# State-space output of a hybrid encoder block, computed transposed in column halves of TensorE

## The chip, the cores and the metric

The kernel runs on one core of a Trainium2 chip. The metric is the device time of one execution in microseconds (us). TensorE (PE, with its weight loads PEld), VectorE (DVE), ScalarE (ACT), GpSimd (POOL) and SyncE (SP, which issues most transfers) run side by side and wait for each other through semaphores.

## The reference

One encoder block over 1024 tokens of width 1024: RMS norm, a product with `w_in`, two groups of heads side by side (a Mamba-2 state-space group, "SSD", and a stick-breaking attention group), a product with `w_out`, norm and residual, then a SwiGLU mixer (`w_gate`, `w_up`, `w_down`). What the change touches is the SSD's output:

```python
y_diag = jnp.einsum("bgcls,bgrcls,bcsgrp->bclgrp", cb, decay_in, x)      # within a block
y_off = jnp.einsum("bclgn,bcgrpn,bgrcl->bclgrp", cc, prev, jnp.exp(a_cs)) # from the state before it
y = y_diag + y_off + d_skip[:, None] * xs
```

There are 8 heads of 64 channels, in two groups of four; a group shares B and C with 128 states. The kernel works in 8 blocks of 128 tokens rather than the reference's 16 of 64, which gives the same sums.

## The kernel before, in words

All arrays are float32. Large products run as three products of split operands (`mm3`, L76 to L78, float32r). The products of the SSD are plain float32, and each appears in the trace as two matmul records and two weight loads.

The program is written as generators. `attention` is one stream of small steps (scores L561 and L562, sigmoids L563 and L564, a scan L567, transposes L578, splits L582 and L583, products with the values L590). `fill` is the other: it goes through `PLAN`, in which tiles of `w_in`'s product (`proj`) alternate with conv tiles, and from "ssd" on it takes one step of `ssd()` behind each step of `proj`. `merge` interleaves the two streams by the costs that each step yields (TensorE us, VectorE us). Program order is only a priority: the framework that builds the kernel orders the instructions of each engine ahead of time by its own model of when each would be ready, and each engine, SP's queue of transfers among them, then runs its list strictly in order. Tiles come from pools with a fixed number of places per tag: `t2` has 8 places of 2 KB for a partition, used by the SSD, by q, k and v on their way to DRAM, by attention's `otmp` and `vld`; the PSUM tag `px` has 3 banks, used by the SSD, attention's transposes and the norms.

`dt_stage` makes, among others, `acs` (running sums of the decay exponents, tokens on partitions), their exponential `E_c`, and a transposed copy `acsT` (rows are block and head, columns are tokens), which goes to DRAM as `acs_d` and comes back broadcast to all partitions as `ab`.

`ssd()` has `front(b)` for a block: it loads `cx` (8 channel tiles of x, B, C by 128 tokens) and the decay matrix `de`, makes C times B in `pcb` (L416), transposes B (L418) and x (L429), multiplies the decay in (`Gm`, L423: per head, source tokens on partitions, target tokens along the free axis) and x by dt (`xdt`, L431: tokens by channels). A block then has three steps. Step A: eight products for `py` (L441, stationary `Gm`, moving 64 columns of `xdt`), `xdc` (L445), two products for `po` (L449, stationary C of a group, moving 256 columns of the state), `y = po * E_c` (L450), `y += py` (L451); the first block has no state and copies `py` with ACT (L453). Step B: `front` of the next block. Step C: the new state (`pst` L460, L463, L467), then `yd = cx * dsk` by four ACT instructions (L473), four transposes of `y` into `pyt` (L476), `yd += pyt` (L477), and the store to `ys_d` (L478). The `z` tiles load `ys_d` later and gate it.

Of the kernel before, what the change touches and what calls it, by code (L numbers as in the profile page):

```python
# [16 lines left out]
P = 128  # L17
S = 1024
# [16 lines left out]
# what in_proj makes, in order; "ssd" from where on SSD's steps run beside the tiles  # L35
PLAN = ('qkv1', 'x0', 'x1', 'x2', 'x3', 'x4', 'x5', 'qkv2', 'x7', 'x6', 'ssd', 'qkv3', 'z0', 'z1', 'r0', 'z2', 'z3', 'wo', 'l1', 'o0')
# how far attention is where the other stream is 0, 1/8, .. 1 done
# [10 lines left out]
def tile_hybrid_block(  # L48
# [15 lines left out]
    """The rows of x and out run backwards in time (row s is token S-1-s), so that every  # L64
    running product over earlier tokens is a forward scan along the free axis."""
# [4 lines left out]
    def split(hi, lo, src):  # L70
        """hi + lo == src, hi and lo each exact in float32r."""
        A.copy(hi, src)  # L72
        V.tensor_tensor(lo, src, f32(hi), ALU.subtract)  # L73
# [6 lines left out]
    # ------------------------------------------------------------------ constants  # L80
# [20 lines left out]
    # TensorE's clock rises with use: products of ones while the first loads run  # L101
# [3 lines left out]
    # tri[s, l] = 1 where s >= l  # L105
    tri = const.tile([P, P], F32, name="tri")
    G.affine_select(tri, ones_f, [[-1, P]], ALU.is_ge, 0.0, base=0, channel_multiplier=1)
    # scan floor: 1 where the key is not strictly before the query, 0 elsewhere
# [3 lines left out]
    # column h is 1 on the 64 partitions of head h of a pair  # L112
# [6 lines left out]
    E_c = const.tile([P, NB, NH], F32, name="E_c")  # L119
# [4 lines left out]
    # DRAM scratch  # L124
    cx_d = dram.tile([8, P, S], F32, name="cx_d")
    dec_d = dram.tile([NB, P, NH * P], F32, name="dec_d")
    acs_d = dram.tile([NB * NH, P], F32, name="acs_d")
    ys_d = dram.tile([4, P, S], F32, name="ys_d")
    y_d = [dram.tile([8, P, 512], F32, name=f"y_d{n}") for n in range(2)]
    # means of squares and what they make 1 / rms: even heads, odd heads, SSD groups  # L130
# [8 lines left out]
    # ------------------------------------------------------------------ right side: x * gain and in_proj weights  # L139
# [4 lines left out]
    # the rows' 1 / rms scales columns here, so it is applied to what comes out of in_proj  # L144
# [13 lines left out]
    # sel16 sums the products of the two halves of w2  # L158
# [11 lines left out]
    # columns of w_in in the order of their use; each tile is loaded and split while the one before it  # L170
    # is multiplied
# [5 lines left out]
    def fetch_w(half=None):  # L177
        """The next column tile, or one half of it."""
# [15 lines left out]
    # ------------------------------------------------------------------ pre-mix norm, first products  # L194
# [40 lines left out]
    # ------------------------------------------------------------------ left side: attention, conv and SSD work  # L235
# [20 lines left out]
    def qkv_tiles(j, st):  # L256
        """What takes q, k (each in its two parts) and v of a pair of heads out of PSUM, to DRAM."""
# [38 lines left out]
    # ------------------------------------------------------------------ dt, decays  # L296
    def dt_stage():
# [18 lines left out]
        # softplus(x) = max(x, 0) + log1p(exp(-|x|)), log1p(e) = 2 atanh(e / (2 + e))  # L316
# [23 lines left out]
        A.activation(E_c, acs, AF.Exp)  # L340
# [6 lines left out]
        nc.sync.dma_start(acs_d, acsT)  # L347
        yield
# [11 lines left out]
        # attention's sigmoids, which need these, wait for the last exponential: ScalarE changes its table once  # L360
# [4 lines left out]
    # ------------------------------------------------------------------ conv tiles  # L365
# [38 lines left out]
    # ------------------------------------------------------------------ SSD  # L404
    def ssd():
# [27 lines left out]

        cur = front(NB - 1)
        yield 1.6, 1.8
        for b in range(NB - 1, -1, -1):
            sl = slice(P * b, P * b + P)
            cx, bs, Gm, xdt = cur
            py = psum("px", "py", [P, 512])
            for h in range(NH):  # L440
                T.matmul(py[:, HD * h : HD * h + HD], lhsT=Gm[:, h, :], rhs=xdt[:, h, :], start=True, stop=True)  # L441
# [4 lines left out]
            if state is not None:  # L446
                po = psum("px", "po", [P, 512])
                for g in range(2):
                    T.matmul(po[:, 256 * g : 256 * g + 256], lhsT=cx[:, 6 + g, :], rhs=state[:, 256 * g : 256 * g + 256], start=True, stop=True)  # L449
# [922 lines left out]
```

## Time and profile before

| | us |
|---|---|
| median of 3 runs | 1248.95 |
| lowest, highest run | 1248.57, 1249.61 |
| span of the profiled execution | 1249.6 |
| TensorE busy in it | 1204.2 (96%) |
| VectorE busy in it | 932.1 (75%) |
| ScalarE busy in it | 587.7 (47%) |

The span is from the first to the last instruction of the profiled execution; it lies at the upper end of the three runs and 0.65 us over their median, so nothing has to be added around it. Busy TensorE time counts pipelined matmuls from start to modelled end, and a busy engine is not one at its peak. The chain of work followed back from the last instruction is 69% TensorE, 14% VectorE and 8% transfers.

### The profile page before, as it was taken

To read this page: it belongs to the slowest core of one execution; us is meant where nothing else is said; L and a number is where in the kernel's file an instruction comes from. 1 tells how busy PE (TensorE), PEld (TensorE's weight loads), DVE (VectorE), ACT (ScalarE), POOL (GpSimd) and SP (SyncE) were. 2 spreads that over 40 slices of the span, in tenths; PEclk is the share of its full clock that TensorE was granted. 3 is DMA by queue.
4 is the path that set the end of the run, shared out by engine and by line. 5 is a ranking of instruction groups with operands and counts; after the bars stand their busy time and mean duration, and the time that the engine had idled before them with its cause. 6 is when DMAs were issued, how large, how long until landed. Compare 5 with 4: busy or idle time off the path is not lost.

```text
span 1249.6 us, 16320 instructions
## 1 busy us (share of the span) xinstructions
PE 1204.2 (96%) x5641; PEld 972.0 (78%) x5641; DVE 932.1 (75%) x1461; ACT 587.7 (47%) x1115; POOL 92.1 (7%) x232
## 2 busy tenths in 40 slices
PE   8998999999999998998799999999999999999997
PEld 7776778787887776787678888888888888888885
DVE  7478988778997887676897565566555558998777
ACT  7347655556655666444653332333233325444543
POOL 0041110010110100011200000000000000000000
PEclk9998999999999999999899999999999999999999
DMA  5693252445466326754872212312132198133336
GB/s 188 194 358 107 67 152 82 142 117 178 142 181 190 118 93 212 228 173 159 271 207 93 93 60 93 101 59 93 52 100 98 58 327 318 62 124 101 102 135 235
DMA packets 139882, 183.23 MB, mean 147 GB/s; under 512 B 10660, under 2 KB 94852, under 8 KB 139800
## 3 DMA queue, kind: packets, MB, share of 16 engines
q1 hardware_dynamic: 128544, 151.18, 38.3%
q0 software_dynamic: 7424, 25.17, 5.5%
q10 hardware_dynamic: 3832, 5.84, 1.3%
q8 instruction: 44, 0.72, 0.2%
q14 instruction: 38, 0.31, 0.1%
HBM read 132.23 MB, written 49.92 MB: 146 GB/s over the span
## 4 chain that ended last, share of the span: by engine, by line
PE 69%; DVE 14%; DMA 8%; issue 4%; ACT 4%; SPq 2%; DVEq 0%; ACTq 0%
PE pd L77 5%; PE pd L76 5%; PE pd L78 5%; DVE sn L567 3%; DMA Rb<-r_d 3%; PE o L590 2%; PE tp L578 2%; PE pj_x L76 2%; PE pj_x L78 2%; PE pcg L76 2%; PE pj_x L77 2%; PE pcu L76 2%; PE peg L76 2%; PE peu L76 2%; PE peu L77 2%
## 5 line engine op out<-in xcount | busy, mean ns | idle before, releaser
L72 ACT CAST flhi<-fraw 128x512 fp32r<-128x512 f32 x102 | 62.7, 622 | 174.1 <-PE pcg L77 37.0
L77 PE MATMUL pd<-folo,fohi 128*128 128x512 f32 x260 | 101.2, 389 | 0.0
L76 PE MATMUL pd<-fohi 128*128 128x512 f32 x260 | 101.2, 389 | 0.0
L78 PE MATMUL pd<-fohi,folo 128*128 128x512 f32 x260 | 101.1, 389 | 0.0
L567 DVE TENSOR_TENSOR_SCAN sn<-sn,smask 128x1024 f32<-128x1024 f32 (+3 forms) x64 | 87.4, 1366 | 17.7 <-ACT sn L563 17.7
L73 DVE TENSOR_TENSOR fllo<-fraw,flhi 128x512 fp32r<-128x512 f32 x102 | 69.6, 686 | 38.9 <-ACT flhi L72 38.5
L72 ACT CAST fohi<-rt 128x512 fp32r<-128x512 f32 x83 | 48.9, 618 | 51.2 <-PE pd L77 30.7
L563 ACT ACTIVATE sn<-zp,msc 128x512 f32<-128x512 f32 (+2 forms) x96 | 56.0, 585 | 34.3 <-PE zp L562 30.6
L582 ACT CAST wh<-tp 128x512 fp32r<-128x512 f32 (+1 forms) x80 | 42.7, 545 | 38.4 <-PE tp L578 37.9
L72 ACT CAST flhi<-fs 128x512 fp32r<-128x512 f32 x44 | 27.2, 622 | 70.4 <-PE peg L77 37.0
L73 DVE TENSOR_TENSOR folo<-rt,fohi 128x512 fp32r<-128x512 f32 x83 | 55.2, 694 | 6.4 <-ACT fohi L72 6.4
L583 DVE TENSOR_TENSOR wl<-tp,wh 128x512 fp32r<-128x512 f32 (+1 forms) x80 | 49.7, 628 | 10.8 <-ACT wh L582 10.3
L564 ACT ACTIVATE sp<-zp,msc 128x512 f32<-128x512 f32 (+2 forms) x96 | 55.8, 584 | 2.5 <-PE tp L578 2.5
L76 PEld LDWEIGHTS pd<-fohi 128*128 128x128 f32 x260 | 48.8, 188 | 10.3
L78 PEld LDWEIGHTS pd<-fohi,folo 128*128 128x128 f32 x260 | 48.8, 188 | 10.1
L77 PEld LDWEIGHTS pd<-folo,fohi 128*128 128x128 f32 x260 | 48.8, 188 | 10.1
L1004 POOL DMA_DIRECT2D a_d<-sg x44 | 23.7, 540 | 392.4 <-DVE sg L1003 392.4
L76 PE MATMUL pj_x<-hh,wh_x 128*128 128x512 f32 x128 | 52.5, 410 | 0.0
L578 PE MATMUL tp<-ident,sp 128*128 128x128 f32 x288 | 47.6, 276 | 5.0 <-DVE sp L568 4.5
L76 PE MATMUL po<-woh,yhl 128*128 128x512 f32 x128 | 51.0, 399 | 1.0 <-ACT yhl L72 1.0
L78 PE MATMUL po<-woh,yhl 128*128 128x512 f32 x128 | 51.0, 400 | 0.6 <-DVE yhl L73 0.5
L78 PE MATMUL pj_x<-hh,wl_x 128*128 128x512 f32 x128 | 51.1, 399 | 0.0
(422 smaller groups left out, 3479.4 us busy)
## 6 DMA issues: line engine op xcount, KB each, us to landing
ps<-a_d SPq DMA_DIRECT2D x55, 256.0 KB
fraw<-in_w_gate_dram SPq DMA_DIRECT2D x22, 512.0 KB
fraw<-in_w_up_dram SPq DMA_DIRECT2D x22, 512.0 KB
a_d<-sg POOLq DMA_DIRECT2D x44, 256.0 KB, 2.5
rt<-in_w_down_dram SPq DMA_DIRECT2D x33, 256.0 KB
rt<-a_d SPq DMA_DIRECT2D x22, 256.0 KB
ps<-in_w_down_dram SPq DMA_DIRECT2D x22, 256.0 KB
xt<-in_x_t_dram SPq DMA_DIRECT2D x8, 512.0 KB
```

The source lines that it names most:

```text
L72: A.copy(hi, src)
L73: V.tensor_tensor(lo, src, f32(hi), ALU.subtract)
L76: T.matmul(ps, lhsT=ah, rhs=bh, start=start, stop=False, skip_group_check=more)
L77: T.matmul(ps, lhsT=ah, rhs=bl, start=False, stop=False, skip_group_check=more)
L78: T.matmul(ps, lhsT=al, rhs=bh, start=False, stop=stop, skip_group_check=more)
L563: A.activation(sn[:, 1 + off : 1 + off + cw_], zp[:, 0:cw_], AF.Sigmoid, scale=rqn[:, qb : qb + 1])
L564: A.activation(sp[:, off : off + cw_], zp[:, 0:cw_], AF.Sigmoid, scale=rqp[:, qb : qb + 1])
L567: V.tensor_tensor_scan(sn[:, 1 : 1 + W], sn[:, 1 : 1 + W], smask[:, 0:W], 1.0, ALU.mult, ALU.max)
L578: T.transpose(tp[:, P * i : P * i + P], ws[a][:, co : co + P], ident)
L582: A.copy(wh[:, 0:n_], tp[:, 0:n_])
L583: V.tensor_tensor(wl[:, 0:n_], tp[:, 0:n_], f32(wh[:, 0:n_]), ALU.subtract)
L590: T.matmul(o[:, 0:cw_], lhsT=vv[:, k, h, :], rhs=wt[:, c0 : c0 + cw_], start=(first and k == kb + 1 and wt is wh), stop=(last and k == kb ...
```

## The change

The output of a block is made with channels on partitions and tokens along the free axis, which is the shape that `yd` has. For each head the stationary operand is now `xdt` of that head (64 columns) and the moving operand is `Gm` (128 columns); the result has 64 partitions, and a pair of heads fills the lower and the upper half of one 128-column slice of the `py` bank. The term from the state is added into the same slice: stationary is the state of the head (64 columns), moving is `cs`, the C of its group times the exponential of `acs` for each target token. `cs` is a product on VectorE of `cx` with a broadcast of `e_d`, which is `exp(acsT)` written to DRAM once in `dt_stage`. `E_c`, `po`, `y`, `pyt`, the two operations on `y`, the ACT copy and the transposes of `y` are gone, and the copies to `yd`, its addition and its store move from step C to step A. The costs that the steps yield to `merge` are rearranged: 2.0 and 2.7 for A, 0.5 and 1.2 for C (before: 1.2 and 1.8, 1.3 and 1.2); the last block yields once in place of twice. Comments are removed elsewhere.

```diff
@@ dt_stage
-        A.activation(E_c, acs, AF.Exp)
         A.activation(dst_c, df, AF.Exp)
         A.activation(cd_c, pc[:, 1], AF.Exp)
...
         nc.sync.dma_start(acs_d, acsT)
+        eT = t2.tile([64, P], F32, tag="t2", name="eT")
+        A.activation(eT, acsT, AF.Exp)
+        nc.sync.dma_start(e_d, eT)
@@ ssd
+        def decayed(b, cx):
+            out = []
+            for g in range(2):
+                cs = t2.tile([P, 4, P], F32, tag="t2", name="cs")
+                r0 = NH * b + 4 * g
+                nc.sync.dma_start(
+                    cs.rearrange("p h l -> p (h l)"),
+                    e_d[r0 : r0 + 4, :].rearrange("h l -> (h l)").partition_broadcast(P),
+                )
+                V.tensor_tensor(cs, cs, cx[:, 6 + g, None, :].to_broadcast([P, 4, P]), ALU.mult)
+                out.append(cs)
+            return out
...
-            py = psum("px", "py", [P, 512])
-            for h in range(NH):
-                T.matmul(py[:, HD * h : HD * h + HD], lhsT=Gm[:, h, :], rhs=xdt[:, h, :], start=True, stop=True)
-            y = t2.tile([P, NH, HD], F32, tag="t2", name="y")
+            xdc = None
             if b > 0:
                 xdc = t2.tile([P, NH, HD], F32, tag="t2", name="xdc")
                 V.tensor_tensor(xdc, xdt, dst_c[:, b, :, None].to_broadcast([P, NH, HD]), ALU.mult)
-            if state is not None:
-                po = psum("px", "po", [P, 512])
-                for g in range(2):
-                    T.matmul(po[:, 256 * g : 256 * g + 256], lhsT=cx[:, 6 + g, :], rhs=state[:, 256 * g : 256 * g + 256], start=True, stop=True)
-                V.tensor_tensor(y, po.rearrange("p (h e) -> p h e", h=NH), E_c[:, b, :, None].to_broadcast([P, NH, HD]), ALU.mult)
-                V.tensor_tensor(y, y, py.rearrange("p (h e) -> p h e", h=NH), ALU.add)
-            else:
-                A.copy(y, py.rearrange("p (h e) -> p h e", h=NH))
-            yield 1.2, 1.8
+            cs = state is not None and decayed(b, cx)
+            py = psum("px", "py", [P, 4, P])
+            for c in range(4):
+                for h in (2 * c, 2 * c + 1):
+                    o = py[HD * (h % 2) : HD * (h % 2) + HD, c, :]
+                    T.matmul(o, lhsT=xdt[:, h, :], rhs=Gm[:, h, :], start=True, stop=state is None, skip_group_check=True)
+                if state is not None:
+                    for h in (2 * c, 2 * c + 1):
+                        o = py[HD * (h % 2) : HD * (h % 2) + HD, c, :]
+                        T.matmul(o, lhsT=state[:, HD * h : HD * h + HD], rhs=cs[h // 4][:, h % 4, :], start=False, stop=True, skip_group_check=True)
+            yd = t2.tile([P, 4, P], F32, tag="t2", name="yd")
+            for c in range(4):
+                A.activation(yd[:, c, :], cx[:, c, :], AF.Copy, scale=dsk[:, c : c + 1])
+            V.tensor_tensor(yd, py, yd, ALU.add)
+            nc.sync.dma_start(ys_d[:, :, sl].rearrange("c p s -> p c s"), yd)
+            yield 2.0, 2.7
...
-            yd = t2.tile([P, 4, P], F32, tag="t2", name="yd")
-            for c in range(4):
-                A.activation(yd[:, c, :], cx[:, c, :], AF.Copy, scale=dsk[:, c : c + 1])
-            pyt = psum("px", "pyt", [P, 4, P])
-            for c in range(4):
-                T.transpose(pyt[:, c, :], y.rearrange("p h e -> p (h e)")[:, P * c : P * c + P], ident)
-            V.tensor_tensor(yd, pyt, yd, ALU.add)
-            nc.sync.dma_start(ys_d[:, :, sl].rearrange("c p s -> p c s"), yd)
-            yield 1.3, 1.2
+                yield 0.5, 1.2
```

## Rows read from the trace of the kernel before

**Rows 1.** The page, its first part: busy time of each engine (share of the span) and its instructions.

```profile
PE 1204.2 (96%) x5641; PEld 972.0 (78%) x5641; DVE 932.1 (75%) x1461; ACT 587.7 (47%) x1115; POOL 92.1 (7%) x232
```

**Rows 2.** Busy time of each engine in five long stretches: start and end of the stretch, its length, then for PE, PEld, DVE, ACT and POOL the busy time and (instructions), the granted clock, the DMA engines' share and GB/s. Attention and the other stream run side by side from 97 to 480, the SSD from 302 to 412.

```profile
97.00:302.00 205.00, 195.86 (x1007) 160.03 (x1008) 175.59 (x214) 123.57 (x225) 22.65 (x76) 0.99 0.38 111
302.00:412.00 110.00, 106.92 (x671) 90.36 (x669) 97.59 (x153) 61.04 (x141) 9.85 (x40) 1.00 0.60 177
412.00:480.00 68.00, 65.04 (x316) 46.87 (x316) 54.17 (x72) 44.21 (x82) 5.29 (x16) 1.00 0.31 105
...
610.00:1210.00 600.00, 592.82 (x2553) 480.33 (x2552) 420.17 (x672) 222.90 (x386) 25.90 (x48) 0.99 0.36 121
```

**Rows 3.** The same view of the SSD's stretch in five parts.

```profile
302.00:312.00 10.00, 9.66 (x57) 7.73 (x55) 6.77 (x10) 4.81 (x10) 0.29 (x1) 1.00 0.85 250
312.00:340.00 28.00, 27.26 (x188) 24.50 (x188) 26.82 (x41) 16.88 (x40) 3.05 (x12) 1.00 0.49 153
340.00:372.00 32.00, 30.56 (x201) 26.47 (x200) 31.68 (x50) 18.77 (x45) 2.85 (x12) 1.00 0.54 165
372.00:400.00 28.00, 27.50 (x155) 21.61 (x153) 20.91 (x37) 11.67 (x27) 2.72 (x11) 1.00 0.79 217
400.00:413.00 13.00, 12.93 (x85) 10.85 (x84) 12.37 (x20) 9.91 (x23) 1.64 (x8) 1.00 0.32 103
```

**Rows 4.** The chain that ended last, from 302 to 413: start, length, what (x instructions merged).

```profile
311.44 1.73 PE py L441 x16
...
313.91 0.45 PE pcb L416 x4
...
317.72 0.44 PE pyt L476 x4
...
321.28 0.92 PE po L449 x4
...
364.29 0.60 DVE y L451
...
373.47 1.73 PE py L441 x16
...
382.92 1.73 PE py L441 x16
...
405.28 0.88 PE py L441 x6
406.38 1.06 PE py L441 x10
```

**Rows 5.** Groups of instructions from 302 to 413, shapes apart: line, engine, operation, out<-in, shape, count | busy us, mean ns of one | idle time of the engine before them and what ended it.

```profile
L441 PE MATMUL py<-xdt,Gm 128*128 128x64 f32 x128 | 15.5, 273 | 0.1
...
L477 DVE TENSOR_TENSOR yd<-pyt,yd 128x512 f32<-128x512 f32 x8 | 5.5, 682 | 0.0
...
L445 DVE TENSOR_TENSOR xdc<-xdt,dst_c 128x512 f32<-128x512 f32 x7 | 4.8, 682 | 0.0
...
L450 DVE TENSOR_TENSOR y<-po,E_c 128x512 f32<-128x512 f32 x7 | 4.8, 681 | 2.1 <-PE po L449 2.1
L451 DVE TENSOR_TENSOR y<-y,py 128x512 f32<-128x512 f32 x7 | 4.7, 677 | 0.0
```

**Rows 6.** The timeline of the weight loads and matmuls around one narrow product (2 columns of weights) from 391.5 to 393.7: start, length of the record, engine, line, operation. Records of matmuls overlap, so the pace is read from start to start.

```profile
391.55 0.39 PE L77 MATMUL pj_z<-hl,wh_z 128*128 128x512 f32 x1
...
391.78 0.39 PE L78 MATMUL pj_z<-hh,wl_z 128*128 128x512 f32 x1
392.09 0.09 PEld L487 LDWEIGHTS nps<-nsq,sel 128*2 128x2 f32 x2 [0.35 <-ACT nsq L484]
392.10 1.02 PE L487 MATMUL nps<-nsq,sel 128*2 128x512 f32 x2
...
393.38 0.40 PE L77 MATMUL pj_z<-hl,wh_z 128*128 128x512 f32 x1
```

**Rows 7.** The same view around the one product with 64 columns of weights that the trace has, at 60 us.

```profile
59.67 0.40 PE L76 MATMUL pj_q<-hh,wh_q 128*128 128x512 f32 x1
59.96 0.27 PE L344 MATMUL pt<-ident,acs 128*64 128x128 f32 x1
...
60.30 0.39 PE L78 MATMUL pj_q<-hh,wl_q 128*128 128x512 f32 x1
```

**Rows 8.** Waits from 302 to 412: who waited for whom, us in total, times, the longest. 

```profile
DVE y L450 <- PE po L449: 2.1, 2, 2.0
...
PEld pcb L416 <- DVE y L451: 1.0, 1, 1.0
...
PE pcb L416 <- DMA cx<-cx_d: 0.3, 1, 0.3
```

**Rows 9.** The timeline from 386 to 397, the loads of one value tile pair and the first instruction that reads them.

```profile
391.36 1.03 SPq L538 DMA_DIRECT2D vld<-v_d  x2
...
396.58 0.60 PE L544 MATMUL pv<-ident,vld 128*128 128x128 f32 x4
```

**Rows 10.** The timeline from 59 to 67, the decays' exponentials and the loads behind them.

```profile
60.26 0.21 ACT L342 ACTIVATE cd_c<-pc 128x64 f32<-128x64 f32 x1
...
61.08 0.60 SPq L530 DMA_DIRECT2D kl<-k_d  x1
...
62.50 0.59 ACT L72 CAST qh<-pj_q 128x512 fp32r<-128x512 f32 x1 [2.03 <-PE pj_q L78]
```

More of the change, by code (lines that the diff above doesn't have):

```diff
@@ L118, in tile_hybrid_block @@
     dt_c = const.tile([P, NB, NH], F32, name="dt_c")
-    E_c = const.tile([P, NB, NH], F32, name="E_c")
     dst_c = const.tile([P, NB, NH], F32, name="dst_c")
@@ L127, in tile_hybrid_block @@
     acs_d = dram.tile([NB * NH, P], F32, name="acs_d")
+    e_d = dram.tile([NB * NH, P], F32, name="e_d")
     ys_d = dram.tile([4, P, S], F32, name="ys_d")
```

## The prediction

> **What bounds the kernel now.** I read from the whole to the place. The page's first part [rows 1] has TensorE busy 96% and VectorE 75% of the span. The stretches [rows 2] show that these are means over different regimes: from 610 to 1210 TensorE is busy 592.8 of 600 us and VectorE 420.2, so that part is TensorE's alone and the change does not touch it. From 97 to 480 attention and the other stream share the core; within it the SSD runs from 302 to 412, where TensorE is busy 106.9 and VectorE 97.6 of 110 us. Cut finer [rows 3], the SSD's stretch is not one regime either: from 312 to 372 VectorE is busy 26.8 + 31.7 = 58.5 of 60 us, nearly full, and so is TensorE (57.8); from 372 to 413 TensorE has 40.4 of 41 and VectorE only 33.3. The chain [rows 4] agrees: it lies on TensorE through `py`, `po` and `pyt` early, is on VectorE around 364, leaves it by the products with the values at 371.6, and then stays on TensorE for the last three `py`, at 373, 383 and 405. So TensorE time saved in the last three of eight blocks should come back in full; time saved in the first five meets a VectorE that has 1.5 us of slack over 60. The waits [rows 8] add what the old form costs in round trips: VectorE waits 2.1 us for `po`, the weight load of `pcb` 1.0 us for the bank that `y` frees.
>
> **TensorE, removed.** `py` is 16 records in 1.73 us, `po` 4 in 0.92, `pyt` 4 in 0.44 [rows 4]. Over the blocks 8 x 1.73 + 7 x 0.92 + 8 x 0.44 = 13.8 + 6.4 + 3.5 = 23.8 us.
>
> **TensorE, added.** Eight products in each of eight blocks and eight more in the seven with a state are 120, with two records each (128 records for the 64 products of `py` [rows 5]) 240 records. Each moves 128 columns against 64 columns of weights. The nearest row for 128 moving columns in float32 is `pcb`, 4 records in 0.45 us, 0.11 each [rows 4]. Note that `py` with 64 moving columns costs the same 0.108: moving fewer columns did not buy anything there. One after another the new records cost 240 x 0.11 = 26.4 us, 2.6 more than what goes. But two heads of a pair use different column halves of the array and different partitions of the bank, and nothing that one makes is read by the other. If the halves work side by side a pair of records takes the time of one; a half-filled array cannot do more work for its time than the full array of `pcb`, so 120 x 0.11 = 13.2 us is the floor. No row shows two narrow products in different columns next to each other, so the two ends stand; the row nearest in shape [rows 7] shows a product with 64 columns of weights between two full ones: from 59.67 to 60.30 is 0.63 us for two full products at 0.23 (the pace in [rows 6]) and it, which leaves 0.17. It is served without a long stop, but it says nothing of two at once. I take side by side, because the order of the records (two of the lower half, two of the upper, two of the lower) always puts a record of the other half next, and the records of neighbouring matmuls already overlap: at a pace of 0.108 they are 273 ns long [rows 4, 5].
>
> Going to narrow products and back costs something. Around `nps`, with 2 columns of weights [rows 6], from 391.78 to 393.38 are 1.60 us: two full products at 0.23 and two records of 512 columns at 4 x 0.11, which leaves about 0.25; in [rows 7] 0.17 less 0.11 leaves 0.06. With one visit for each block this is 8 x 0.06 = 0.5 at the least; with three for each block with a state 22 x 0.25 = 5.5 at the most. I take two for each of the seven and one for the first, 15 x 0.2 = 3.0, since the matmuls of the state can stand behind `cs` while others are let in between. [...]
>
> TensorE's sum: 13.2 + 3.0 - 23.8 = -7.6 us side by side, between 13.2 + 0.5 - 23.8 = -10.1 and, one after another, 26.4 + 3.0 - 23.8 = +5.6, at worst 26.4 + 5.5 - 23.8 = +8.1. The price of a record at which nothing is gained is (23.8 - 3.0) / 240 = 0.087 us.
>
> **VectorE.** Seven `y = po * E_c`, seven `y += py` and eight `yd += pyt` [rows 5] are 22 operations of 0.68 us. Fourteen `cs` and eight `yd += py` are 22 again. The trace has no `cs`; its nearest row is `xdc`, two operands from SBUF at 128x512, 0.682 [rows 5], the same as `y` from PSUM at 0.681. So 0 us; were `cs` a tenth dearer, 14 x 0.07 = 1.0 us more. ACT loses a copy of one block, under a us, off the chain.
>
> **Moved.** The four ACT copies, the addition to `yd` and the store go ahead of the next `front`. The store is then issued by SP before the loads of `cx` and `de` of that front instead of after them; they are 8 + 8 loads that the schedule places some microseconds ahead, and I cost this at nothing as long as it does. `cx` is free a step earlier, and `px` gives four banks for each block where it gave six; both can only take away waits such as the 1.0 us of `pcb` on `y` [rows 8]. Where VectorE is full these waits are hidden behind it, so I count none of it.
>
> **Transfers.** New are 14 loads of 256 KB, 3.7 MB, in a stretch where the transfer engines are busy 0.60 at 177 GB/s over 110 us [rows 2], that is 19.5 MB; a fifth more, to about 0.7. They go through SP and need a place in `t2`, of which a block now takes five for four. The nearest row is `vld`, two loads of the same 256 KB into the same pool: issued at 391.36, first read at 396.58, 5.2 us later [rows 9], without a wait shown; TensorE waits 0.3 us for a transfer in the whole stretch [rows 8]. I take 0: a load waits for nothing but its place, so it can be issued while VectorE still works for the step before. If that cover goes, VectorE stands at `cs` with attention's scans and splits behind it, and TensorE behind those.
>
> In `dt_stage` one exponential and one store are added and one exponential goes. ACT is done at 60.47 and waits 2.03 us until 62.50; SP is done with the load before at 61.68 [rows 10]. Both fit; at worst the loads of `ab` behind them start an issue later, 0.5 us.
>
> **From TensorE's sum to the span.** Of -7.6 us three eighths fall in the last three blocks, where TensorE alone is full: -2.9. In the five others VectorE's slack allows 1.5. Together -4.4 us: 1249.6 - 4.4 = 1245.2 against the profiled execution, or 1244.6 against the median of 1248.95. Its own bounds: with all of 10.1 saved, 3.8 + 1.5, and 2 us of work pulled forward into later stretches, 1241.6; with 5 visits' worth more and no slack used, about 1247.
>
> **The rivals.**
> *One after another.* The array gives a narrow product its full time whatever half it uses. Place: the 15 groups of new products. For it: a record of 64 moving columns costs no less than one of 128 [rows 4], so records have a floor that halves need not beat. Against it: the overlap of records. It decides from 0.087 us for each record on. Price: +5.6 on TensorE, which has only 110 - 106.9 = 3.1 us of gaps there, many of them waits; taking 1.1 off for the round trips that go, +4.5, so 1253.5, slower.
> *VectorE holds the stretch.* TensorE's saving becomes waiting for scans and splits through all blocks, since VectorE's 22 operations stay. For it: 58.5 of 60 us [rows 3]. Against it: 7.7 us of slack from 372 to 413. It gives -0.5 or so, 1248.4.
> *The loads of `cs` come late.* If SP gets to them only as the step comes, they need up to the 5.2 us of `vld`; with 2 us seen by VectorE in each of seven blocks, 14 us, less 4.4 gained: 1258.5. It decides from a wait of 4.4 / 7 = 0.6 us for each block. Against it: the small waits of today.
> *Weight loads bare.* Each weight load, not hidden by a running matmul, would add at least the 0.09 / 2 us that two loads of 2 columns show in [rows 6]; 240 x 0.045 to 240 x 0.09 on top of the serial price is +16 to +27, some 1270. Against it: in [rows 6] both loads of `nps` lie in the first 0.09 us while its matmuls take 1.02, so the second ran ahead beside the first matmul. [...]
>
> **How the numbers follow.** Side by side with part of it realized 0.48, one after another 0.22, VectorE holds 0.17, late loads 0.10, bare loads 0.03. A measurement of this kernel can tell about 0.2% or 2.5 us from no change, so faster means under 1246.4 and slower over 1251.5. Faster: 0.45 of the first, 0.02 of VectorE holds, 0.01 of the serial case with many waits gone: 0.48. Slower: 0.16 of the serial case, 0.08 of late loads, 0.03 of bare loads, 0.02 of VectorE holds with dearer `cs`: 0.29. The rest, 0.23, is the same. The likeliest case gives 1244.6, with a range of its own from 1241.6 to 1247. The range over all cases goes from 1239.5, a little beyond the best of the first, to 1256, which leaves out the bare loads, the worse part of the late ones and the extreme serial price.
>
> **What would show it.** Starts of the sixteen records of `py` at 0.055 us on average show side by side, 0.11 one after another, 0.15 or more bare loads. Stops of 0.1 to 0.25 around each group show the visits. VectorE's count in the stretch should stay, `cs` at 0.68. A row "DVE cs waits for DMA" over 4 us in total shows late loads; TensorE less than 90 of 100 busy from 312 to 372, with VectorE at 98, shows that VectorE holds. The prediction fails most easily if the built order changes around the SSD so that other steps, not these, move the stretch.

## The result: slower by 0.31%

The changed kernel takes 1253.82 us (median of 16 runs, 1251.42 to 1258.2) against 1250.38 us of the kernel before on the same chip: a ratio of 1.0031, with a 95% interval of 1.0020 to 1.0041. By that ratio it is 3.9 us more (the two medians differ by 3.4), where 4.4 less were predicted.

The two profiled executions have spans of 1249.7 and 1249.6 us and so hide the difference. Single executions of one kernel lie up to 3 us below and 4 us above the median, and the profiled one of the new form was the shortest of its 16 runs (1251.42 us, 1.7 more than its span). Spans can't be compared at this size, but stretches between two marks can, with the limits given below the table. Four marks stand in every trace: the store of `acs_d` at 60 us, the first loads of `cx` (the SSD begins), the first loads of `ys_d` back as `yt` (it is nearly done), and attention's last product with the values. SP's timeline has the middle two, first of the kernel before and then of the new form; in the new form they are 113.1 us apart instead of 111.7:

```profile
302.50 1.12 SPq L411 DMA_DIRECT2D cx<-cx_d  x2
...
414.23 0.81 SPq L498 DMA_DIRECT2D yt<-ys_d  x2
```

```profile
303.94 1.14 SPq L413 DMA_DIRECT2D cx<-cx_d  x2
...
416.99 0.82 SPq L511 DMA_DIRECT2D yt<-ys_d  x2
```

For all kernels that ran, in us: A is from the store of `acs_d` to the loads of `cx`, B from there to the loads of `yt`, C from there to attention's last product. The ratio is to the kernel before on the same chip, with its interval.

| kernel | A | B | C | A+B+C | ratio |
|---|---|---|---|---|---|
| before | 241.9 | 111.7 | 69.4 | 423.0 | 1 |
| the change | 244.3 | 113.1 | 69.1 | 426.5 | 1.0031 [1.0020, 1.0041] |
| e1: old products, new decay stage | 244.4 | 110.9 | 69.4 | 424.7 | 1.0019 [1.0004, 1.0035] |
| e2: new, no loads of `cs` | 244.2 | 106.8 | 70.4 | 421.4 | 0.9998 [0.9983, 1.0014] |
| e3: new, no loads, old decay stage | 241.6 | 107.0 | 70.5 | 419.1 | 0.9977 [0.9963, 0.9992] |
| e4: new, one half, then the other | 246.8 | 123.4 | 64.2 | 434.3 | 1.0081 [1.0056, 1.0107] |
| e5: new, loads on GpSimd's queue | 244.0 | 121.8 | 69.1 | 434.8 | 1.0103 [1.0083, 1.0123] |
| e6: new, store on ScalarE's queue | 242.1 | 113.3 | 69.1 | 424.5 | 1.0011 [0.9998, 1.0025] |
| e7: e5 and e6 together | 242.4 | 118.9 | 69.8 | 431.1 | 1.0085 [1.0068, 1.0102] |
| e8: new, loads unread | 244.4 | 109.4 | 69.6 | 423.4 | 1.0016 [1.0003, 1.0028] |
| e9: e8, an eighth of the bytes | 244.5 | 109.0 | 70.4 | 423.9 | 1.0007 [0.9997, 1.0017] |
| e10: decay on the output | 242.7 | 109.4 | 70.0 | 422.0 | 1.0008 [0.9996, 1.0020] |
| e11: new, store and loads on ScalarE | 242.8 | 118.2 | 65.4 | 426.5 | 1.0057 [1.0036, 1.0077] |
| e12: e10, loads early, on ScalarE | 242.9 | 106.5 | 71.5 | 420.9 | 1.0004 [0.9990, 1.0018] |
| e13: e12 without its loads | 243.1 | 107.7 | 70.9 | 421.7 | 0.9995 [0.9981, 1.0009] |
| e14: e10, loads early, on SP | 242.6 | 108.4 | 70.6 | 421.7 | 1.0003 [0.9988, 1.0017] |

Kernels whose instructions stand in the same order agree within 0.2 to 0.8 us in B (e2 and e3; the change and e6; before and e1), so a difference of 2 us there is one. The row of the kernel before may be some 0.8 long in B, as e1 says. A is 244.0 to 244.5 with the store of the exponentials on SP's queue (e4 stands out with 246.8) and 241.6 to 243.1 without it; kernels with the same order up to the SSD spread over 1 us there. B and C have to be read together, because work can cross the mark between them. From the second mark to the fourth, the change, e2, e3 and e8 run the same number of instructions on VectorE and ScalarE and, within one, on TensorE. The rows have start and end, length, then busy time and (instructions) of PE, PEld, DVE, ACT and POOL, the granted clock (a share of full speed), the transfer engines' share and GB/s: first before, then the change, e8, e2 and e3.

```profile
302.50:483.61 181.11, 173.60 (x998) 138.63 (x996) 154.87 (x231) 108.36 (x226) 15.14 (x56) 1.00 0.49 152
```

```profile
303.94:486.10 182.16, 171.13 (x1052) 128.09 (x1050) 153.92 (x231) 108.02 (x225) 16.35 (x56) 1.00 0.57 171
```

```profile
304.71:483.67 178.96, 171.00 (x1051) 127.78 (x1050) 153.78 (x231) 107.95 (x225) 18.38 (x56) 1.00 0.57 174
```

```profile
303.86:481.12 177.26, 170.01 (x1052) 128.67 (x1051) 153.42 (x231) 108.16 (x225) 16.43 (x56) 1.00 0.51 155
```

```profile
303.74:481.28 177.54, 170.15 (x1051) 128.55 (x1050) 153.39 (x231) 108.15 (x225) 16.71 (x56) 1.00 0.51 155
```

Length less busy time is TensorE's idle time: 7.5 us before, 11.0 in the change, 8.0 in e8, 7.2 in e2 and 7.4 in e3.

**TensorE did as predicted.** TensorE's timeline in the new form: start, length of the group with its overlap, records.

```profile
313.19 1.09 PE L465 MATMUL py<-Gm,xdt 128*64 128x128 f32 x16
314.22 0.39 PE L603 MATMUL o<-wl,vv 128*128 128x256 f32 x1
...
327.50 0.39 PE L465 MATMUL py<-Gm,xdt 128*64 128x128 f32 x4
327.72 0.39 PE L469 MATMUL py<-cs,state 128*64 128x128 f32 x4
327.94 0.39 PE L465 MATMUL py<-Gm,xdt 128*64 128x128 f32 x4
```

Four records, two heads, from start to start in 0.22 us: 0.055 each. Sixteen take 1.03 with what a visit costs, where the old `py` took 1.73 [rows 4]. Less 16 x 0.055 that leaves 0.15 for the visit. The groups of `cs` and of the narrow weight loads from 302 to 420 (busy us, mean ns of one | idle time before them), and the busy times that answer to [rows 2, 3]:

```profile
L446 DVE TENSOR_TENSOR cs<-cs,cx 128x512 f32<-128x512 f32 x14 | 9.6, 701 | 0.5 <-DMA cs<-e_d 0.4
L465 PEld LDWEIGHTS py<-Gm,xdt 128*64 128x64 f32 x128 | 7.5, 136 | 1.7 <-issue 1.3
```

```profile
302.00:412.00 110.00, 104.51 (x726) 81.34 (x726) 94.56 (x151) 61.25 (x141) 11.03 (x41) 1.00 0.71 208
...
312.00:340.00 28.00, 27.16 (x192) 21.79 (x191) 27.42 (x42) 19.91 (x47) 3.53 (x13) 1.00 0.63 190
340.00:372.00 32.00, 30.05 (x232) 24.10 (x232) 31.55 (x51) 16.31 (x38) 3.45 (x11) 1.00 0.61 189
372.00:400.00 28.00, 27.16 (x175) 19.41 (x174) 18.03 (x33) 11.07 (x27) 1.39 (x6) 1.00 0.91 248
```

TensorE has 5.5 us of gaps from 302 to 412 where it had 3.1. From 372 to 400 VectorE does less than before (18.0 us for 20.9) while the transfer engines are at 0.91 for 0.79: something waits there, and it isn't for VectorE's capacity.

**Where the time went.** First, in the decay stage. SP's timeline of the new form (the store of the exponentials stands between that of `acs_d` and a load of keys) and ScalarE's, some 35 us later:

```profile
59.65 0.46 SPq L346 DMA_DIRECT2D acs_d<-acsT  x1
60.21 0.54 SPq L349 DMA_DIRECT2D e_d<-eT  x1
60.80 0.65 SPq L543 DMA_DIRECT2D kl<-k_d  x1
```

```profile
96.16 0.62 ACT L72 CAST wh_x<-wr_x 128x512 fp32r<-128x512 f32 x1 [3.71 <-DMA wr_x<-in_w_in_dram]
...
98.09 0.69 ACT L576 ACTIVATE sn<-zp,msc 128x512 f32<-128x512 f32 x1
```

In the kernel before the same cast stood behind the first sigmoids:

```profile
96.62 0.69 ACT L563 ACTIVATE sn<-zp,msc 128x512 f32<-128x512 f32 x1
...
105.08 0.64 ACT L72 CAST wh_x<-wr_x 128x512 fp32r<-128x512 f32 x1
```

From the store of `acs_d` to the first sigmoid are 36.05 us before and 38.44 in the new form, 2.4 more: one cast that waits 3.71 us for its weights now stands ahead of attention's sigmoids. Second, around the SSD. Waits from 302 to 417 in the new form, those of SP in front of loads of `cs` last, and SP's timeline where attention changes to its next pair of heads:

```profile
DVE vv L559 <- ACT vv L558: 7.7, 2, 7.3
PEld py L469 <- DVE cs L446: 3.6, 5, 1.5
PE py L469 <- DVE cs L446: 1.8, 3, 1.0
DVE cs L446 <- DMA cs<-e_d: 0.4, 1, 0.4
```

```profile
SPq L442 <- DMA ss_d<-ss: 3.3, 1, 3.3
SPq L442 <- PE pst L481: 2.0, 2, 1.8
SPq L442 <- PE zp L575: 1.9, 1, 1.9
```

```profile
379.14 2.50 SPq L442 DMA_DIRECT2D cs<-e_d  x2
...
385.59 0.52 SPq L543 DMA_DIRECT2D kl<-k_d  x1
387.67 0.33 SPq L260 DMA_DIRECT2D v_d<-vr  x1
389.74 0.38 SPq L474 DMA_DIRECT2D ys_d<-yd  x1
390.21 0.46 SPq L610 DMA_DIRECT2D y_d<-osb  x1
390.71 0.46 SPq L542 DMA_DIRECT2D kh<-k_d  x1
...
392.33 0.45 SPq L543 DMA_DIRECT2D kl<-k_d  x1
```

With 1.0 us for a store of `v` and 0.2 for ScalarE, SP stands 8.4 us in front of loads of `cs`, and what is behind them in its list stands with it. The 2.50 us at 379.14 hold one such wait: two issues of 0.32 us each, and 1.8 us for TensorE's `pst` between them. The last keys of the pair stand behind three stores, and SP waits for VectorE in front of the first two. Before, SP had issued all keys by 383.4, ahead of the store of `v` at 387.72:

```profile
377.56 0.60 SPq L529 DMA_DIRECT2D kh<-k_d  x1
...
382.85 0.52 SPq L530 DMA_DIRECT2D kl<-k_d  x1
...
387.72 0.34 SPq L260 DMA_DIRECT2D v_d<-vr  x1
```

### The profile page after: what moved, and what is told of

It is laid out like the page before. It is cut to its first block, busy times and chain, and to the rows that moved or that the text cites. A ratio compares the mean times of both kernels' runs of the same rounds, so it can differ in the third digit from the quotient of the medians.

```text
span 1249.7 us, 16460 instructions
## 1 busy us (share of the span) xinstructions
PE 1199.2 (96%) x5693; PEld 961.2 (77%) x5693; DVE 927.5 (74%) x1461; ACT 587.5 (47%) x1114; POOL 94.4 (8%) x232
## 4 chain that ended last, share of the span: by engine, by line
PE 68%; DVE 14%; DMA 7%; issue 5%; ACT 4%; SPq 1%; POOL 0%; DVEq 0%; ACTq 0%; POOLq 0%
PE pd L77 5%; PE pd L78 5%; PE pd L76 5%; DVE sn L580 3%; DMA Rb<-r_d 2%; PE pcg L76 2%; PE peu L76 2%; PE pcg L77 2%; PE peg L77 2%; PE peu L78 2%; PE peg L76 2%; PE pcg L78 2%; PE pcu L78 2%; PE peu L77 2%; PE peg L78 2%
## 5 line engine op out<-in xcount | busy, mean ns | idle before, releaser
L73 DVE TENSOR_TENSOR fllo<-fraw,flhi 128x512 fp32r<-128x512 f32 x102 | 69.4, 683 | 38.2 <-ACT flhi L72 38.2
L76 PE MATMUL po<-woh,yhl 128*128 128x512 f32 x128 | 51.3, 401 | 2.9 <-ACT yhl L72 2.9
L581 DVE TENSOR_TENSOR sp<-sp,sn 128x1024 f32<-128x1024 f32 (+3 forms) x64 | 48.0, 753 | 3.8 <-POOL sp L579 1.4
```

Of the source, the lines that this page charges most:

```text
L76: T.matmul(ps, lhsT=ah, rhs=bh, start=start, stop=False, skip_group_check=more)
L581: V.tensor_tensor(sp[:, 0:W], sp[:, 0:W], sn[:, 0:W], ALU.mult)
```

## The experiments

**e1: the decay stage alone.** The kernel before with the exponential and its store added.

```diff
         nc.sync.dma_start(acs_d, acsT)
+        eT = t2.tile([64, P], F32, tag="t2", name="eT")
+        A.activation(eT, acsT, AF.Exp)
+        nc.sync.dma_start(e_d, eT)
```

> The kernel before with only the new part of dt_stage: the exponential eT and its store to e_d, which nothing reads (E_c stays). Theory one, the dt part: in the two traces the kernel after is 0.9 us ahead when acs_d is stored (59.65 against 60.57) and 1.4 us behind from 121 to 302, so this part costs about 2.3 us, a ratio of 1.0018, and the shift stands from 121 on. Theory two, the loads of cs: the dt part costs nothing, 1.000.

Measured 1.0019, as theory one said, A 244.4 against 241.9, B not longer. 32 KB that nothing reads cost 2.4 us, in front of the SSD.

**e2 and e3: the new products without loads, and with the old decay stage too.**

```diff
-                nc.sync.dma_start(... e_d ...)
-                V.tensor_tensor(cs, cs, cx[:, 6 + g, None, :]..., ALU.mult)
+                V.tensor_tensor(cs, ones_f[:, None, :]..., cx[:, 6 + g, None, :]..., ALU.mult)
```

> The kernel after without the 14 loads of cs: cs is C times one, so the decay of the state's term is left out of the output; eT and e_d are still made. Theory two, the loads of cs: in the trace of after SP reaches the last load of the next keys (kl) at 392.33 where before had it at 382.85, and VectorE idles 7.3 us behind it; without the loads the time falls by 4 to 7 us against after, to 0.997 to 1.000 of before. Theory one, the dt part: it falls by at most 1.5 us, to about 1.002. Third theory, VectorE holds the stretch and the visits of the narrow products eat the rest: it stays at 1.003.

> As the run without the loads, and eT and e_d left out too: only the new arithmetic is left, and up to the SSD the order of every engine is that of before. Theory one: 2.3 us less than the run without the loads. If both theories hold: -4.4 us against before, the gain that the prediction worked out, 0.9965. Third theory: 1.000 or slower.

Both leave the decay of the state's term out of the output. Measured 0.9998 and 0.9977. So the products alone win 0.23%, 2.9 us (1.0 to 4.6 by the interval); the decay stage takes 0.21% and the loads 0.33%, 4.1 us. The intervals of the change and of e2 do not touch; those of e2 and e3 overlap a little, and there A decides, 244.2 against 241.6. In the traces e3 is 4.7 us shorter than the kernel before in B and 1.1 longer in C, 3.6 shorter in both.

**e4: one half of the array, then the other.**

```diff
-            for c in range(4):
-                for h in (2 * c, 2 * c + 1):
+            for h in (0, 2, 4, 6, 1, 3, 5, 7):
```

> The kernel after with the products ordered by halves: the four heads of the lower half first, then the four of the upper, so that neighbours share a half; the output is the same. If halves work side by side only because neighbours differ, records come at 0.11 us in place of 0.055 and TensorE has 13 us more to do in the stretch: if TensorE's time counts there, 5 to 9 us slower than after (1.007 to 1.010 of before); if VectorE holds the stretch, within 2 us of after.

Measured 1.0081, a further 0.5%, as expected if TensorE's time counts. TensorE's timeline of it, where records of one half follow each other:

```profile
330.84 0.38 PE L464 MATMUL py<-Gm,xdt 128*64 128x128 f32 x2
331.06 0.38 PE L466 MATMUL py<-cs,state 128*64 128x128 f32 x2
331.28 0.38 PE L464 MATMUL py<-Gm,xdt 128*64 128x128 f32 x2
```

Two records for 0.22 us in place of four: 0.11 each, the price of the full array. The same instructions, only in another order, so the halves do work side by side in the change, and TensorE's time counts. It is not the slice of the bank that decides: in the block without a state, where neighbours write different slices, the sixteen records of e4 last from 316.50 to 318.02, 1.5 us for 1.03 in the change. (2.5 of the added us stand in A, where the order is that of the change. 1.4 of them come ahead of the first sigmoid, where the cast of a weight tile waits 4.60 us for its load. The rest comes from 135 to 145, behind a gap of TensorE of 2.0 us that both traces have: the granted clock has a mean of 0.83 there, and 1.00 in the change.)

**e5, e6 and e7: other queues.** One word each, and both.

```diff
-                nc.sync.dma_start(cs...
+                G.dma_start(cs...            # e5, e7
-        nc.sync.dma_start(e_d, eT)
+        A.dma_start(e_d, eT)                 # e6, e7
```

> The new form with one word changed: the 14 loads of cs are issued on GpSimd's queue instead of SP's; the same bytes, the same places, the same products. The program order of the loads of keys and values on SP then has no cs entries between them. Theory one (the loads cost because they stand in SP's list ahead of attention's keys, 379.14 in the trace of the new form, with the pair's last keys at 390.7 and 392.3 where the old form has them at 377.6 and 382.9): the keys come back to before 385, VectorE's wait for vv of 7.7 us goes, and the ratio to the kernel before falls from 1.0031 to about 1.0000, as with the loads left out (0.9998). Theory two (the 3.7 MB themselves slow the other transfers, the DMA share of 0.91 from 372 to 400): the queue does not matter, 1.003. Theory three (GpSimd's masks of attention now wait behind loads that wait for a place): 1.005 or more, and VectorE waits for sp or sn from GpSimd.

> The new form with one word changed in the decay stage: the store of the exponentials (e_d, 32 KB) is issued on ScalarE's queue instead of SP's. The built order of all engines is then that of the kernel before up to the SSD, with the one exponential and the store added on ScalarE. Theory one (the 2.4 us of the decay stage come from the built order: a cast of a weight tile that waits 3.7 us for its load stands ahead of attention's first sigmoids): that cast goes back to about 105 us, the first zp waits 3.5 us as before, and the ratio falls by 0.0019 to 0.0021, from 1.0031 to 1.0010. Theory two (the exponential and the small store cost by themselves, wherever they stand): 1.003. Rival: the order ahead of the SSD is that of the kernel before, but what it gains is lost again in the SSD's stretch: the trace is 1.4 us ahead at 302 and not at 417.

> Both one-word changes together: loads of cs on GpSimd's queue, store of the exponentials on ScalarE's. If both causes are queue order and add up, this is what the new arithmetic is worth with its data brought in without disturbing the rest: 0.9977 to 0.9985, 1246.9 to 1247.9 us, faster than the kernel before, near the run without loads and decay (0.9977). If the loads cost by their bytes, 1.001. If GpSimd's queue turns into a new wait, above 1.002.

e6 came as theory one said: 1.0011, A back at 242.1, the cast at 103.47 behind the sigmoids. From the store of `acs_d` to the first sigmoid are 36.3 us again. So the 2 us of the decay stage come from where the store on SP's queue puts other instructions in the built order; the exponential and the store are still there. The wait of the cast itself is not the whole price: in e2, e8 and e9 it is 1.6 to 2.2 us and the first sigmoid 1.1 to 1.5 late, A is the same, and the rest is lost from 130 to 140, where the granted clock has a mean of 0.83 and the change 1.00. (e7 and e10 to e14 have the order of e6 up to the SSD and 242.4 to 243.1 in A, so up to 1 us of all this is not settled.) e5 came as its third theory said: 1.0103. Its waits from 302 to 417:

```profile
DVE cs L446 <- DMA cs<-e_d: 10.8, 7, 5.0
PEld py L469 <- DVE cs L446: 7.2, 7, 2.2
POOL cs L442 <- DVE cs L446: 6.1, 1, 6.1
```

GpSimd's list holds attention's masks too. The loads stand behind masks that wait for ScalarE (47.0 us in 16 waits), and arrive too late; one load waits 6.1 us for its place, with masks behind it. The granted clock is lower too, and whether that follows from the waits is not shown. TensorE is busy 1.5 of the 6 us from 388 to 394, and from 394 to 396 its clock is 0.50; from 302 to 417 the mean is 0.97, where the change has 1.00:

```profile
390.00:392.00 2.00, 0.00 (x0) 0.00 (x0) 0.92 (x2) 0.00 (x0) 0.00 (x0) 1.00 0.13 51
...
394.00:396.00 2.00, 2.00 (x15) 1.24 (x11) 1.68 (x4) 0.63 (x1) 0.00 (x0) 0.50 0.77 221
```

So e5 tells nothing about SP, and e7 repeats it at 1.0085, 0.18% lower with the store on ScalarE's queue.

**e8 and e9: loads that nobody waits for, at full size and an eighth.**

```diff
+                cl = t2.tile([P, 4, P], F32, tag="t2", name="cl")
-                    cs.rearrange(...), e_d[...].partition_broadcast(P),
+                    cl.rearrange(...), e_d[...].partition_broadcast(P),        # e8
+                    cl[0:16].rearrange(...), e_d[...].partition_broadcast(16), # e9
```

> The new form with the 14 loads kept on SP's queue, into places of their own that nothing reads, while cs is C times a tile of ones (the decay of the state's term is left out of the output). Nothing waits for the loads; they only take their entries in SP's list, their places in the pool and their share of the transfer engines. Theory one (entries in SP's list) and theory two (bytes): it stays near the new form, 1.002 to 1.004, although VectorE waits for none of them. Theory three (VectorE's wait for the arrival of cs is the cost): it comes down to 0.9998, the run without loads.

> As the kernel with unread loads, with each load cut to 16 of its 128 partitions (32 KB for 256 KB): the same 14 entries at the same places of SP's list, the same order on every engine, an eighth of the bytes; cs is again C times a tile of ones, so the decay of the state's term is left out. Theory one (entries in SP's list, and their waits for a place in the pool): it stays with the unread loads of full size, 1.0016. Theory two (bytes): it falls to the run without loads, 0.9998, and the loads of attention's keys behind these entries are issued in 0.45 to 0.6 us each and not in up to 1.6. The two sit 0.0018 apart, which is close to what the intervals of two runs can tell.

1.0016 and 1.0007, between the change and e2, where no theory had put them; the interval of e9 holds both of its forecasts. Every engine's order is the same in both, and is neither that of the change nor that of e2. B is 109.4 and 109.0, B and C together 179.0 and 179.4: the marks show no price of the bytes, and the ratios differ by 0.0009 within their intervals. Over e2, the 14 entries and what they reorder make 1.7 to 2.1 us in B and C together (179.0 and 179.4 less 177.3), and another 3.2 up to 182.2 come only when `cs` is read. By the ratios these parts have the same sign but lie within each other's intervals. Of the 3.2, 3.1 are idle time of TensorE (11.0 us less 8.0). It waits 1.8 us for `cs`, and 1.1 longer than in e8 for `wl`, attention's splits on VectorE; the change is first, then e8, between the second mark and the fourth:

```profile
PE o L603 <- DVE wl L596: 4.0, 8, 1.2
```

```profile
PE o L604 <- DVE wl L597: 2.9, 5, 1.2
```

What the entries alone do shows in VectorE's wait, first in e9 and then in e3:

```profile
DVE vv L560 <- ACT vv L559: 6.7, 1, 6.7
```

```profile
DVE vv L551 <- ACT vv L550: 1.4, 2, 1.1
```

With an eighth of the bytes VectorE still stands 6.7 us at `vv`: its list has the scans behind `vv` that stood ahead of it in e3. Yet TensorE is busy 27.46 of the 28 us from 372 to 400 in e9, as before (27.50), and e9 as a whole is 0.0009 over e2, 1.1 us: a long wait of an engine that is not the bound there.

**e10 to e14: a better version.** The decay goes on the result of the state's products, where one tile of 128 by 512 for a block holds it; the products wait for no load. In e10 to e14 the store of the exponentials is on ScalarE's queue.

```diff
-                        T.matmul(o, lhsT=state[:, HD * h : HD * h + HD], rhs=cs[h // 4][:, h % 4, :], start=False, ...)
+                E2 = decays(b)          # e12 to e14: in front(b), behind the load of de
+                po = psum("px", "po", [P, 4, P])
+                for c in range(4):
+                    T.matmul(po[:, c, :], lhsT=state[:, P * c : P * c + P], rhs=cx[:, 6 + c // 2, :], start=True, stop=True)
+                V.tensor_tensor(E2, po, E2, ALU.mult)      # e13: po times ones, no loads
+                V.tensor_tensor(yd, yd, E2, ALU.add)
```

> A version made from what the other runs say. The store of the exponentials is on ScalarE's queue. The decay is no longer multiplied into C ahead of the state's products (two tiles of 256 KB for a block) but into their result: with channels of a pair of heads on partitions one tile of 128 by 512 holds it, loaded as two times 128 KB, half the bytes. The state's products become four full ones of 128 by 128 for a block in a bank po of their own, which wait for no load; py has the eight products within the block alone. VectorE does po times E2, yd plus py and yd plus that: three operations for a block with a state, as the new form. Same output. TensorE: 128 narrow records at 0.055 and 56 full ones at 0.11, 13.2 us as the new form, with eight visits to narrow products for fifteen. Theory (the loads cost by bytes and by TensorE's wait for them): 0.9978 to 0.9995, faster than the kernel before, against 1.0011 for the form with the two loads. Rival (the extra bank of px, or VectorE's three operations in a row at the end of a step, hold the next step): 1.001 to 1.003.

> The new form with two words changed: both the store of the exponentials and the 14 loads of cs are issued on ScalarE's queue; same bytes, places, products and output. In the built order SP's list has attention's last keys of the pair ahead of the stores of v, yd and the attention's output again, as in the kernel before, and VectorE has four scans and masks ahead of the operation vv. So far every kernel with entries for these loads on SP (the new form, the store on ScalarE, unread loads of full and of small size, the decay on the output) shows VectorE waiting 6.7 to 7.7 us for vv between 390 and 398, and every kernel without them (before, and the two without loads) 1.1 to 1.4. Theory one (that order is the larger part of the loads' price): the wait is 1.5 us or less, and the ratio to the kernel before is 0.9980 to 1.0000 (the store moved gives 1.0011, the wait 5 to 6 us less, of which the kernel gets back 1.5 to 4). Rival one (waits of a load for its place or for its entry now hold ScalarE's sigmoids and copies): 1.0015 or more, with waits of ScalarE on VectorE's cs or of VectorE on the loads of cs above 4 us. Rival two (the bytes): 1.0005 to 1.0015 with the wait for vv gone.

> The version with the decay on the output, its half-size loads issued on ScalarE's queue and a step earlier, beside the loads of cx and of the decay matrix of the block. Same output. SP's list and VectorE's at the pair's end stand as in the run without loads and decay. Theory one: the wait for vv is 1.5 us or less and the ratio is 0.9975 to 0.9990, faster than before, the decay on the output on SP having 1.0008. Rival one (ScalarE held by a load that waits for a place in the pool): 1.001 or more, and a wait in front of an issue on ScalarE. Rival two (the third operation of VectorE in a row, or the bank po): 1.0000 to 1.0010 with both waits gone.

> The version with the decay on the output with its loads taken away: po is multiplied by a tile of ones, so the decay of the state's term is left out of the output; the exponential and its store on ScalarE's queue stay. Seen from the start of the loads of cx to the first load of ys_d back, the version with loads on ScalarE took 106.5 us, the run without loads and decay 106.8 to 107.0, the kernel before 111.7 and the run with the old products and the new decay stage 110.9. Theory one (the half-size loads on ScalarE cost nothing): this run takes 106 to 107 us there as well and has the same time, 1.0004, within 0.0015, and the 5 us won in the stretch do not reach the end in either. Theory two (the loads cost behind the stretch, through the order of ScalarE or of the later loads): 0.9975 to 0.9990.

> The same version with its half-size loads on SP's queue, a step earlier than in the first version with the decay on the output: beside the loads of cx and of the decay matrix. Same output. ScalarE has no loads, VectorE's built order has its scans ahead of vv, but two of the pair's last keys stand behind a store of v again. If entries on SP's queue cost by pushing the keys behind stores, the stretch from the loads of cx to the first load of ys_d takes 107.5 to 109.5 us (109.4 with the loads a step later, 106.5 with them on ScalarE), and the ratio is 1.0000 to 1.0010; if it was only the operation vv placed ahead of the scans, 106.5 to 107 us and as fast as the version with its loads on ScalarE, or 0.9980 to 1.0000 if issues on ScalarE cost there.

e11 is the change itself with its loads on ScalarE: the wait for `vv` fell to 2.6 us, but it has 1.0057, and the wait of VectorE for the loads is over the 4 us that rival one named:

```profile
PEld py L469 <- DVE cs L446: 8.6, 9, 1.6
...
DVE cs L446 <- DMA cs<-e_d: 6.5, 6, 1.7
```

The version with the decay on the output missed its forecast at 1.0008 with loads on SP, and so did e12 at 1.0004: it has B as short as without any load (106.5), and is not faster than the kernel before. e13 tells that its loads are not the reason: without them 0.9995, the same within the intervals. e14 puts them back on SP with VectorE's scans ahead of `vv`: B 108.4, as theory one said, and 1.0003. VectorE's long wait is still there, now in front of a scan, so it goes with late keys (the last is issued at 387.5, in e12 at 380.3) and not with the place of `vv`:

```profile
DVE sn L576 <- ACT sn L572: 6.9, 1, 6.9
```

So the versions with the decay on the output beat the change by 0.2 to 0.3%, and none beats the kernel before. e13 has no loads either, only the store on ScalarE's queue, and still is 2.6 us over e3 by the marks, 1.5 of it in A; why is open.

## Why the prediction was wrong

**The step that failed is the one on transfers.** "I take 0: a load waits for nothing but its place." The runs put 4.1 us there by the ratio, 5.1 by the marks (426.5 less 421.4). With them and the decay stage the predicted gain turned into a loss; without either, e3 has the gain. The rival "the loads of `cs` come late" had the right sign for the wrong reason: VectorE waited 0.4 us for them, not 4. The price arose in two other ways. The loads do wait for their places, and SP stands 8.4 us in front of them (4.3 in e8), and the last load of the pair's keys, behind them, is issued at 392.33, in the kernel before at 382.85; with the new order of SP's and VectorE's lists around 14 more entries this makes 1.7 to 2.1 us in B and C where nothing reads the loads. And TensorE waits for VectorE's `cs`, which is late by its place in VectorE's list and not by its load (3.2 more, 3.1 of it idle time of TensorE; 1.8 of this is named as `cs` and 1.1 as `wl` behind it).

**The decay stage** was priced by what ScalarE and SP had free, 0.5 us at worst. It costs 2.2 to 2.6 (A of e6, e1 and e2 less e3), 35 us behind the place of the edit, where the order of a cast and a sigmoid flipped. I had written that the forecast fails "if the built order changes around the SSD"; it did, and around the decay stage too, and I gave it no price.

**TensorE's sum was right**: 0.055 a record, side by side. The 240 records stand in 17 groups, which last 16.1 us from their first start to the next other record, against 13.2 + 3.0. That is 0.17 a visit on average; the upper price of 0.25 was misread, as it holds a wait of 0.35 for ScalarE that the line in [rows 6] names. VectorE's 22 for 22 was right too: `cs` has a mean of 701 ns for 14. The -4.4 for the products stands against -2.9 by e3's ratio and -3.6 in B and C, inside e3's interval; its split into 2.9 from three blocks and 1.5 from five was not measured. C is 1.0 to 2.1 us longer in all five kernels with B under 109. In e3 0.9 of its 1.1 are idle time of TensorE (5.3 us for 4.4); where that comes from is not shown. What the change moves (copies, addition and store a step earlier) stands in all of them and was not tried by itself. **VectorE holds** did not come by its sign: TensorE kept 57.2 of 60 us from 312 to 372. But VectorE is busy 59.0 of 60 us there in the change and 59.7 in e3, so the limit that the forecast took for the first five blocks is real. The measured 1253.82 lies next to the 1253.5 of **one after another** by accident: that rival's sign, 0.11 a record, shows only in e4. **Bare weight loads** did not come either: four loads of 0.136 us each pass in 0.22 beside four records.

**The base** was off as well. I took it that nothing lies around the span; the runs of the new form show 1.7 us around it. So the profiled execution of before took about 1251.3 us, inside the 1247.3 to 1254.5 of its 16 runs, and 2.4 above the median I started from, not 0.65. That does not change the sign of anything.

## What to carry to other kernels

An added load or store was more than its bytes here: an exponential and a store of 32 KB that nothing reads took A from 241.9 to 244.4 us (e1), and loads with an eighth of the bytes left B and C together at 179.4, for 179.0 with all of them (e9, e8). It is an entry in a list, and where a framework orders the lists ahead of time it can flip pairs of instructions far away (35 us here); compare the built orders of every engine before and after, and look for a wait that moved ahead of work. Put a small new transfer on a queue whose list does not change the others, as the store on ScalarE's did (e6, A 242.1 for 244.3), but not on one whose own work waits, as GpSimd's does (e5, 1.0103), and ScalarE's did with the 14 loads of e11 (1.0057). To judge 0.3% by traces, compare stretches between marks that all kernels have and that hold the same instructions, not spans.

## What was not expected of the hardware

Products of different column halves next to each other ran at 0.055 us a record with their weight loads (the change), and at 0.11 where the neighbour was in the same half (e4): of the two kernels only the order of the records differs. One of SP's 14 issues of `cs` took 2.12 us, at 331.72 in the new form, with the transfer engines at 0.90 meanwhile. The others took 0.32 to 0.54, among them two of 0.34 and 0.38 at 399, where the transfer engines were at 1.07 from 399 to 401, so their load alone does not make it. And after attention's end TensorE waits for the split inputs of the output product (`po` for `yhl`) 1.0 us in the trace of before and 4.2 in that of e1, with the same order there: single executions differ by some 3 us in one place that this edit does not touch.
